# One decoder layer on one core: transposes in PSUM banks of their own, first partial products in scratch tiles, and new list priorities

## The chip, the core and the metric

The kernel runs on one core of a Trainium2 chip. A core has five engines that work side by side, each through its own list of instructions, in order: TensorE (PE in the profile: matrix products and transposes; its weight loads are counted as PEld), VectorE (DVE), ScalarE (ACT), GpSimd (POOL) and SyncE (SP, which here only issues transfers). TensorE writes to PSUM, which has eight banks of 128 x 512 float32; the other engines read it from there. The metric is the device time of one execution in microseconds (us), and the median of three runs is what is compared.

## The reference

The layer takes x (1024 tokens x 1024 channels, float32) and computes

```
h = rms_norm(x) ; z = h @ w_in                  # 2840 columns: q, 6 x (k or v), gates, hc, cg, bg
k_cmp, v_cmp = compress(kc), compress(vc)       # 32-token blocks, stride 16: gelu(blk @ w1 + b1) @ w2 + b2
attn = nsa_attention(q, k_cmp, v_cmp, ks, vs, kw, vw, sigmoid(gates))   # three branches, 8 heads, 2 groups
conv = bg * causal_conv3(cg * hc)               # short gated convolution, 512 channels
x = x + concat(rms_norm(attn), rms_norm(conv)) @ w_o
x = x + square(relu(rms_norm(x) @ w_up)) @ w_down
```

## The kernel before, in words

Every float32 product is three TensorE products of operands split into a high and a low part (`mm3`: high x high, low x high, high x low). So each operand needs an ACT copy (the high part, names in h or `hTh`, `w_hi`, `w1h`, `wcuh`, `MCh`, `KH`) and a DVE subtraction (the low part, `hTl`, `w_lo`, `w1l`, `wcul`, `MCl`, `KL`), and each result in PSUM has to be drained by ACT or DVE before its bank is used again.

The order of the instructions is not that of the code. A planner (`class Plan`) records every operation with what it needs, gives each a modelled cost (`cost`, L288) and a priority (the longest modelled path from it to the end, plus whatever `plan.plus` holds while the operation is written down, L348), and then lists for each engine what is ready first and has the highest priority. For a transfer the model takes its bytes. All instructions are then issued from one line, L268, so the line tells nothing in this profile and the rows are told apart by the names of their tiles: `out<-in`.

PE's stages in this order: norm and transposes of x, and the k/v columns of z (to 77 us); the q columns (`zp`, eight 512-wide PSUM results, each in w_hi/w_lo pieces) mixed with the compression (`compress_steps`: the loads `ch<-kv_d`, the transposes `tp<-ident,ch`, `araw`, `ah`/`al`, and `hp`, the 16 x 3 products with the streamed first weight `w1h`/`w1l`, whose raw tiles `w_raw<-in_w_cmp` have two buffers) to 131 us; a 280-wide rest of z to 156 us; the convolution's channels (`channels`, `u_pair`: a Strassen-like scheme with seven products over the PSUM results `zX`, `zZ`, `zW`, and the weight sums `wcr`, `wcs`) to 277.5 us. There the first products `A11` and `S2` are copied by ACT into the two halves of the tile `u`, and a DVE addition completes them later. Then `wc`, the convolution half of the output projection (`hTh`/`hTl` hold split rows of w_o there, `MCh`/`MCl` the convolution's result): for each of eight blocks of 128 tokens two 512-wide results, each 12 products, drained by DVE with the factor `rconv` (the convolution's norm, from the column sums `s_<-ones,sqs`) onto a tile that x was loaded into: `y` tiles for six blocks, the single buffer `xt` (pool `xq`, bufs=1) for the first two, from where POOL stores them to `x_d` before `xt` is loaded a second time. Mixed with these stand the transposes of the normed keys (`tp<-ident,kn`, split to `KH`/`KL`), those of the queries (`tpq`) and the first scores. From 337 us on: attention, its projection, and the feed-forward part.

PSUM: to the end of the convolution the pool `psB` has five banks under the tag "mm" (z, hp, zX, zZ, zW) and three under "tr" (transposes). Then `psB` is closed, and `psP` (three banks, transposes), `psS` and `psC` (`wc`: tags "ot" x2 and "ms") are opened in its place; a new tile there waits for whatever used the bank last.

Of the kernel before, what the change touches and what calls it, by code (L numbers as in the profile page):

```python
# [9 lines left out]
F32 = mybir.dt.float32  # L10
# [3 lines left out]
ALU = mybir.AluOpType  # L14
# [4 lines left out]
P = 128  # L19
# [131 lines left out]
class Plan:  # L151
# [133 lines left out]
    last_pe = None  # L285
    plus = 0.0
    follow = ()
    LINK = .05  # L288
    GROUP = 1

    def cost(self, name, method, a, kw, views):
        self.port = False
        n = max([v.cols() for _, v in views], default=1)
        psum = any(v.base.pool.psum for k, v in views if k not in ("out", "accum_out"))
        if method == "dma_start":
            nb = 4 * max(int(np.prod(v.shadow.shape)) for _, v in views)
            return (.58 if name == "POOL" else .33), 0.0, nb
        if name == "PE":
            if method == "transpose":
                c = .109  # L300
            else:
                rhs = a[2]
                c = rhs.cols()
                c = max(4 * c / 4560, .218) if rhs.base.args[1] == F32 else max((c if c >= 256 else 4 * c) / 2400 + .014, .109)
            return c, c + .17, 0
        near = not psum
        if name == "ACT":
            c = (.1 if near else .05) + n * .000834
            if any(isinstance(kw.get(k), View) for k in ("scale", "bias")):
                c += .09  # L310
            acc = kw.get("accum_out") is not None
            return max(c, .17) + .093 * acc, max(c, .17) + .11 + .093 * acc, 0
        if name == "DVE":
            if method == "tensor_tensor_reduce":
                return .163 + n * .00104, .26 + n * .00104, 0
            if method == "scalar_tensor_tensor":
                c = .1 + n * .0011 if n >= 200 else .11 + n * .0012
            elif method == "tensor_scalar":
                c = .06 + n * .00059 + (.05 if n < 64 else 0)
            elif method == "memset":  # L320
                c = .08 + n * .0005
            else:
                c = .064 + n * .00104
            self.port = near and n >= 64
            return c, c + .08, 0
        self.port = n >= 64
        if method == "tensor_tensor":
            if kw.get("op") == ALU.pow:
                return .4 + .15 * n, .45 + .15 * n, 0
            c = .15 + n * .00213  # L330
            return c, c + .05, 0
        if method in ("iota", "affine_select"):
            self.port = False
            return .08 + n * .001, .13 + n * .001, 0
        c = .15 + n * .0009 if method == "tensor_copy" else .12 + n * .0008
        return c, c + .05, 0
# [158 lines left out]
def trunk_layer(ctx, tc, x, g_mix_norm, w_in, g_q, g_k, pe_cmp, w_cmp1, b_cmp1, w_cmp2, b_cmp2,  # L495
# [85 lines left out]
    gk_bc = twp.tile([P, 3, HD], F32, name="gk_bc")  # L581
    TD = {n: [htp.tile([P, 4, 512], F32R, name=f"{n}{q}") for q in "hl"] for n in ("t1", "t2")}
    wp = pool(wp_stack, "wp", bufs=4, side="right")
    psB_stack = ExitStack()
    psB = pool(psB_stack, "psB", bufs=5, space=PSUM)

# [25 lines left out]
    with ExitStack() as a:  # L612
# [9 lines left out]
        nc.sync.dma_start(rows[24:36], conv_w.rearrange("j (k p) -> (j k) p", p=P))  # L622
        nc.sync.dma_start(rows[36:68], pe_cmp.rearrange("k (q two) d -> (k q) (two d)", two=2))
        plan.plus = 0.0
        tp = psB.tile([P, 512], F32, name="tp", tag="tr", bufs=3)
        nc.tensor.transpose(tp[:, :68], rows, ident[:68, :68])
        nc.vector.tensor_copy(cols, tp[:, :68])
        def norm_in(tb):
            xt = xts[tb]
            junk = xp.tile([P, D], BF16, name="junk", tag="junk", bufs=1)  # L630
            ss = st.tile([P, 1], F32, name="ss")
            nc.scalar.activation(junk, xt, AF.Square, accum_out=ss)
            ri = st.tile([P, 1], F32, name="ri")
            rsqrt(ri, ss, 1, 1.0 / D)
            nc.vector.tensor_scalar(xt, xt, ri, None, op0=ALU.mult)
            for half in range(2):
                tp = psB.tile([P, 4, P], F32, name="tp", tag="tr", bufs=3)
                for j in range(4):
                    k = half * 4 + j
                    nc.tensor.transpose(tp[:, j], xt[:, k * P:(k + 1) * P], ident)  # L640
                d = (slice(None), slice(half * 4, half * 4 + 4), slice((tb % 4) * P, (tb % 4 + 1) * P))
                split_psum(hTh[tb // 4][d], hTl[tb // 4][d], tp)
# [17 lines left out]
    def z_tokens(pieces, tbs, n, steps=iter(()), per=0):  # L660
        pss = [psB.tile([P, 512], F32, name="zp", tag="mm") for _ in tbs]
        for j, (wh, wl) in enumerate(pieces):
            for ps, tb in zip(pss, tbs):
                t = slice((tb % 4) * P, (tb % 4 + 1) * P)
                for i in range(2):
                    k = 2 * j + i
                    mm3(ps[:, :n], hTh[tb // 4][:, k, t], hTl[tb // 4][:, k, t], wh[:, i], wl[:, i],
                        k == 0, k == KD - 1)
            for _ in range(per):
                plan.plus = 20  # L670
                next(steps, None)
                plan.plus = 0.0
        return list(zip(tbs, pss))
# [44 lines left out]
    with ExitStack() as b1:  # L718
# [40 lines left out]
        def compress_steps():  # L759
            for kv in range(2):  # L760
                yield
                ch = cp.tile([P, 16, HD], F32, name="ch")
                for g in range(G):
                    c0 = kv * G * HD + g * HD
                    nc.sync.dma_start(ch[g * 64:(g + 1) * 64],
                                      kv_d[:, c0:c0 + HD].rearrange("(i p) d -> i p d", p=16))
                A = {}
                for half in range(2):
                    A[half] = (cp.tile([P, 8, P], F32R, name=f"ah{half}"), cp.tile([P, 8, P], F32R, name=f"al{half}"))
                for q4 in range(2):  # L770
                    yield
                    tp = psB.tile([P, 4, P], F32, name="tp", tag="tr", bufs=3)
                    for j in range(4):
                        pp = q4 * 4 + j
                        nc.tensor.transpose(tp[:, j], ch[:, 2 * pp:2 * pp + 2], ident)
# [32 lines left out]
                nc.vector.tensor_scalar(hx, hx, 0.5, None, op0=ALU.mult)  # L808
                nc.vector.scalar_tensor_tensor(hx, th, 1.0, hx, op0=ALU.add, op1=ALU.mult)
                yield  # L810
                tp = psB.tile([P, 4, P], F32, name="tp", tag="tr", bufs=3)
                for j in range(2):
                    nc.tensor.transpose(tp[:, j], hx[:, j * P:(j + 1) * P], ident)
                hT = cp.tile([P, 2, P], F32, name="hT", tag="th")
# [48 lines left out]
                tt(nc.vector, qg[:, :, 1 - g], zg, qg[:, :, g].bitcast(F32), ALU.subtract)  # L863
            nc.sync.dma_start(q_d[tb * P:(tb + 1) * P], qn.rearrange("p h a d -> p (h a d)").bitcast(F32))

        plan.plus = 20
        for _ in steps:
            pass
        plan.plus = 0.0
# [20 lines left out]
    with ExitStack() as b2:  # L890
# [13 lines left out]
        def channels(c0, c1):  # L904
            A = {}
            for j in range(2):
# [7 lines left out]
                for k in range(4):  # L914
                    copy_act(raw[:, k], raw[:, k], scale=cols[:, G_MIX + 4 * j + k:G_MIX + 4 * j + k + 1])
                A[f"A1{j + 1}"], A[f"A2{j + 1}"] = raw[:, :, 0], raw[:, :, 1]
            PART = {"A11": ("b11", "X"), "S1": ("t1", "Z"), "S2": ("t2", "X"), "A12": ("b21", "W"),
                    "S3": ("b12", "X"), "S4": ("b22", "Z"), "A22": ("t4", "X")}
            ps = {}
            for name, (b, chain) in PART.items():  # L920
                hi, lo = [wc.tile([P, 4, P], F32R, name=f"wcu{q}", bufs=3) for q in "hl"]
                copy_act(hi, A[name])
                tt(nc.vector, lo, A[name], hi.bitcast(F32), ALU.subtract)
# [6 lines left out]
                if name == "A12":  # L930
                    tt(nc.vector, A["A12"], A["A12"], A["S2"], ALU.subtract)
                    A["S4"] = A["A12"]
                if chain not in ps:
                    ps[chain] = psB.tile([P, 512], F32, name="z" + chain, tag="mm")
                bh, bl = TD[b]
# [5 lines left out]
        def u_pair(c):  # L941
# [2 lines left out]
            nc.vector.memset(u[:, 0:2], 0.0)  # L944
            for name, ps in channels(C_CONV + c * P, C_CONV + CW + c * P):
                if name == "A11":
                    copy_act(u0, ps)
                elif name == "A12":
                    tt(nc.vector, u0, ps, u0, ALU.add)
                elif name == "S2":  # L950
                    copy_act(u1, ps)
                elif name == "S1":
                    a = half_tile("ca")
                    copy_act(a, ps)
                elif name == "S3":
                    tt(nc.vector, a, ps, a, ALU.add)
                elif name == "S4":
                    tt(nc.vector, u1, ps, u1, ALU.add)
                    tt(nc.vector, u1, u1, a, ALU.mult)
                else:  # L960
                    tt(nc.vector, u0, ps, u0, ALU.mult)
# [59 lines left out]
        for c in range(4):  # L1021
# [4 lines left out]
                copy_act(hi[:, j], r[:, j], scale=g)  # L1026
                nc.vector.scalar_tensor_tensor(lo[:, j], r[:, j], g, hi[:, j].bitcast(F32), op0=ALU.mult, op1=ALU.subtract)
            pieces.append((hi, lo))
        tpk = psB.tile([P, 4, P], F32, name="tpk", tag="tr", bufs=3)
        nc.tensor.transpose(tpk[:, 0], kcn, ident)  # L1030
        wc_stack.close()
        ht_stack.close()
# [39 lines left out]
        def k_transposes(g, br, qd):  # L1072
# [3 lines left out]
            c0 = NCMP + br * T + qd * 512  # L1076
            split_keys(g, c0, 512, tp.rearrange("p a b -> p (a b)"))

        for g in range(G):
            split_keys(g, 0, NCMP, tpk[:, 0, g * 64:(g + 1) * 64])  # L1080
        psB_stack.close()
        cps_stack, psP_stack = ctx.enter_context(ExitStack()), ctx.enter_context(ExitStack())
        psP = pool(psP_stack, "psP", bufs=3, space=PSUM, side="right")
        psC = pool(cps_stack, "psC", space=PSUM, side="right")
        psS_stack = ExitStack()
        psS = pool(psS_stack, "psS", bufs=2, space=PSUM)
# [112 lines left out]
        kts = [(i % 2, i // 2 % 2, i // 4) for i in range(8)]  # L1199
        for i in range(4):  # L1200
            k_transposes(*kts.pop(0))
        for it, tb in [*enumerate(ORDER)][6:] + [*enumerate(ORDER)][:6]:
            xt = xq.tile([P, D], F32, name="xt") if it >= 6 else y_tile([P, D], f"y{tb}")
            nc.sync.dma_start(xt, x2d[tb * P:(tb + 1) * P])
            t = slice(tb * P, (tb + 1) * P)
            for nh in range(2):
                n = slice(nh * 512, (nh + 1) * 512)
                tag, bufs = (("ot", 2), ("ot", 2), ("ms", 1))[(it * 2 + nh) % 3]
                ps = psC.tile([P, 512], F32, name="wc", tag=tag, bufs=bufs)
                for c in range(4):  # L1210
                    wh, wl = pieces[c]
                    mm3(ps, MCh[:, c, t], MCl[:, c, t], wh[:, nh], wl[:, nh], c == 0, c == 3)
# [478 lines left out]
```

## Time and profile before

| | |
|---|---|
| runs | 1247.05, 1249.01, 1251.22 us; median 1249.01 |
| profiled execution | 1247.95 us, of which the span from the first to the last instruction is 1246.2 |
| PE busy | 1210.3 us of the span, 97% |
| DVE, ACT, POOL busy | 927.8, 713.5 and 706.6 us |
| PE waits of over 0.15 us named in the waits view | about 30 us over the whole span |
| mean granted TensorE clock | 0.997 |

The span is about as long as PE's work; a time is read here as PE's busy time and the gaps between its instructions. A gap is put down to the event that came last before the waiting instruction began ("releaser"). [...]

### The profile page before, as it was taken

How to read it: one execution, taken by the hardware profiler on the slowest of the kernel's cores; microseconds unless marked ns; L12 is line 12 of the kernel's file. 1: busy time of each engine (PE TensorE's matmuls, PEld its weight loads, DVE VectorE, ACT ScalarE, POOL GpSimd, SP SyncE). 2: the span in 40 equal slices, each digit the busy share in tenths (PEclk: the TensorE clock that was granted, in tenths of full speed). 3: DMA queues.
4: the chain of work that ended last, by engine and by line, in shares of the span. 5: the costliest groups of instructions: out<-in, count | busy, mean ns of one | idle time of the engine just before them, and what ended most of it. 6: DMA issues, size and time to landing. Idle time of an engine off the chain costs nothing.

```text
span 1246.2 us, 18370 instructions
## 1 busy us (share of the span) xinstructions
PE 1210.3 (97%) x5970; PEld 996.8 (80%) x5970; DVE 927.8 (74%) x1784; ACT 713.5 (57%) x1586; POOL 706.6 (57%) x629
## 2 busy tenths in 40 slices
PE   7989999999989999999999999999999999999998
PEld 6868978777868888888788888888888788888786
DVE  6947766774498789898876665665658999898874
ACT  7557854552388788787956555555344444444440
POOL 2435410011235554333768777877889999888860
PEclk9999999999999999999999999999999999999999
DMA  6265622138121100001225534445349545554413
GB/s 242 64 152 176 179 59 68 42 93 257 58 93 43 38 31 35 27 18 37 100 93 177 178 121 166 135 145 178 136 146 402 184 163 170 168 169 120 134 43 135
DMA packets 105175, 155.01 MB, mean 124 GB/s; under 512 B 20404, under 2 KB 59400, under 8 KB 105080
## 3 DMA queue, kind: packets, MB, share of 16 engines
q1 hardware_dynamic: 102008, 146.05, 36.2%
q10 hardware_dynamic: 2304, 5.24, 1.1%
q0 software_dynamic: 768, 2.56, 0.7%
q8 instruction: 47, 0.77, 0.3%
q14 instruction: 48, 0.39, 0.1%
HBM read 106.63 MB, written 47.19 MB: 123 GB/s over the span
## 4 chain that ended last, share of the span: by engine, by line
PE 75%; DVE 6%; DMA 5%; ACT 5%; issue 3%; POOL 2%; SPq 0%; ACTq 0%; DVEq 0%; POOLq 0%
PE X L268 24%; PE Z L268 15%; PE tp L268 5%; PE ot L268 4%; PE zX L268 4%; PE wa L268 4%; PE wc L268 3%; PE W L268 3%; PE zp L268 2%; PE zZ L268 2%; DMA wu<-in_w_up_dram 2%; PE zW L268 1%; DVE y L268 1%; PE hp L268 1%; POOL d L268 1%
## 5 line engine op out<-in xcount | busy, mean ns | idle before, releaser
L268 PE MATMUL X<-we,uu 128*128 128x512 f32 x720 | 179.5, 390 | 2.0 <-DVE y L268 2.0
L268 PEld LDWEIGHTS X<-we,uu 128*128 128x128 f32 x720 | 134.5, 188 | 32.2 <-ACT uu L268 3.0
L268 PE MATMUL Z<-we,uu 128*128 128x512 f32 x576 | 146.4, 390 | 0.0
L268 ACT ACTIVATE uu<-ur 128x512 fp32r<-128x512 f32 x108 | 66.7, 630 | 121.2 <-PE X L268 58.3
L268 PEld LDWEIGHTS Z<-we,uu 128*128 128x128 f32 x576 | 107.5, 188 | 24.2 <-issue 1.1
L268 ACT ACTIVATE pt<-pt,nm 128x640 f32<-128x640 f32 (+7 forms) x128 | 93.8, 736 | 27.6 <-DVE nm L268 27.1
L268 PE MATMUL tp<-ident,pt 128*128 128x128 f32 x528 | 103.4, 273 | 1.4 <-DVE pl L268 1.1
L268 POOL TENSOR_TENSOR d<-d 128x512 f32<-128x512 f32 x64 | 98.2, 1555 | 10.1 <-DVE d L268 8.1
L268 ACT ACTIVATE ph<-tp 128x512 fp32r<-128x512 f32 (+1 forms) x148 | 82.1, 575 | 31.4 <-PE tp L268 29.0
L268 DVE TENSOR_TENSOR pl<-tp,ph 128x512 fp32r<-128x512 f32 (+1 forms) x148 | 94.7, 654 | 7.2 <-ACT ph L268 6.7
L268 DVE TENSOR_TENSOR y<-X,y 128x512 f32<-128x512 f32 x128 | 79.6, 680 | 13.6 <-PE X L268 13.5
L268 POOL TENSOR_TENSOR uu<-ur,uu 128x512 fp32r<-128x512 f32 x54 | 77.6, 1442 | 12.4 <-DVE y L268 8.7
L268 DVE TENSOR_TENSOR uu<-ur,uu 128x512 fp32r<-128x512 f32 x54 | 72.1, 1349 | 13.1 <-ACT uu L268 12.5
L268 DVE TENSOR_TENSOR we<-s,we 128x512 fp32r<-128x512 f32 x42 | 38.5, 916 | 57.5 <-PE Z L268 25.0
L268 PEld LDWEIGHTS tp<-ident,pt 128*128 128x128 f32 x528 | 68.6, 140 | 13.7 <-POOL pt L268 1.4
L268 DVE TENSOR_TENSOR y<-Z,y 128x512 f32<-128x512 f32 x96 | 61.3, 682 | 19.7 <-PE Z L268 19.6
L268 ACT ACTIVATE wu<-wu,cols 128x256 f32<-128x256 f32 x128 | 55.7, 502 | 24.0 <-DMA wu<-in_w_up_dram 23.5
L268 ACT ACTIVATE we<-wu 128x512 fp32r<-128x512 f32 x57 | 35.9, 631 | 57.5 <-PE X L268 43.9
L268 DVE SCALAR_TENSOR_TENSOR d<-d 128x512 f32<-128x512 f32 x48 | 65.2, 1359 | 0.8
L268 POOL IOTA d_sw<- 128x640 f32 (+1 forms) x2 | 1.2, 609 | 113.3 <-PE zZ L268 113.3
L268 PE MATMUL zp<-w_lo,hTh 128*128 128x512 f32 (+1 forms) x192 | 62.0, 368 | 0.3 <-DVE w_lo L268 0.3
L268 POOL TENSOR_TENSOR pt<-pt,rr 128x640 f32<-128x640 f32 (+4 forms) x64 | 62.3, 1004 | 0.0
(1333 smaller groups left out, 3689.7 us busy)
## 6 DMA issues: line engine op xcount, KB each, us to landing
u_d<-d SPq DMA_DIRECT2D x112, 256.0 KB, 3.2
ur<-u_d SPq DMA_DIRECT2D x108, 256.0 KB, 2.9
wu<-in_w_up_dram SPq DMA_DIRECT2D x16, 1024.0 KB, 6.1
wd<-in_w_down_dram SPq DMA_DIRECT2D x16, 1024.0 KB, 6.3
xt<-in_x_dram SPq DMA_DIRECT2D x10, 512.0 KB, 4.9
w_raw<-in_w_in_dram SPq DMA_DIRECT2D x8, 512.0 KB, 5.9
w_raw<-in_w_cmp_dram SPq DMA_DIRECT2D x16, 256.0 KB, 3.0
q_d<-qn SPq DMA_DIRECT2D x8, 512.0 KB, 3.1
```

Source lines behind the costliest of these rows:

```text
L268: node.do.append(lambda: getattr(engine, method)(*[real(x) for x in a], **{k: real(x) for k, x in kw.items()}))
```

## The change

Six edits, none of which adds or removes an instruction. (1) While the two `ch` loads of each compression are recorded, the planner takes their bytes 2.4 times (`drag`). (2) The pool `psP` with three banks is opened at the start and all transposes take their bank from it until the end of the attention; `psB` is left with five. (3) The compression steps that are written between the q pieces have `plan.plus` 6 in place of 20, and so has what is left of them at the end. (4) The weight loads, sums and splits in `channels` have `plan.plus` 6 in place of 0. (5) `A11` and `S2` go to scratch tiles `ta` and `tb`, one buffer each, and the completing additions read these. (6) The first split of compressed keys has `plan.plus` 20, and the first two `wc` results (the two halves of one token block) take banks of `psP`.

```diff
@@ cost
-            return (.58 if name == "POOL" else .33), 0.0, nb
+            return (.58 if name == "POOL" else .33), 0.0, int(nb * self.drag)
@@
+    psP_stack = ctx.enter_context(ExitStack())
+    psP = pool(psP_stack, "psP", bufs=3, space=PSUM, side="right")
     psB_stack = ExitStack()
     psB = pool(psB_stack, "psB", bufs=5, space=PSUM)
@@ the transposes of rows, x, ch, hx and kcn alike
-                tp = psB.tile([P, 4, P], F32, name="tp", tag="tr", bufs=3)
+                tp = psP.tile([P, 4, P], F32, name="tp", tag="pt")
@@ z_tokens, and again where the rest of the steps is written
-                plan.plus = 20
+                plan.plus = 6
                 next(steps, None)
@@ compress_steps
+                    plan.drag = 2.4
                     nc.sync.dma_start(ch[g * 64:(g + 1) * 64],
                                       kv_d[:, c0:c0 + HD].rearrange("(i p) d -> i p d", p=16))
+                    plan.drag = 1.0
@@ channels
+            plan.plus = float(6)
             PART = {"A11": ("b11", "X"), "S1": ("t1", "Z"), "S2": ("t2", "X"), "A12": ("b21", "W"),
...
             for name, (b, chain) in PART.items():
+                plan.plus = float(6)
...
+                plan.plus = 0.0
                 if chain not in ps:
@@ u_pair
                 if name == "A11":
-                    copy_act(u0, ps)
+                    t0 = wc.tile([P, 512], F32, name="ta", bufs=1)
+                    copy_act(t0, ps)
                 elif name == "A12":
-                    tt(nc.vector, u0, ps, u0, ALU.add)
+                    tt(nc.vector, u0, ps, t0, ALU.add)
                 elif name == "S2":
-                    copy_act(u1, ps)
+                    t1 = wc.tile([P, 512], F32, name="tb", bufs=1)
+                    copy_act(t1, ps)
...
-                    tt(nc.vector, u1, ps, u1, ALU.add)
+                    tt(nc.vector, u1, ps, t1, ALU.add)
@@ after the convolution
+        plan.plus = 20.0
         for g in range(G):
             split_keys(g, 0, NCMP, tpk[:, 0, g * 64:(g + 1) * 64])
+        plan.plus = 0.0
         psB_stack.close()
-        cps_stack, psP_stack = ctx.enter_context(ExitStack()), ctx.enter_context(ExitStack())
-        psP = pool(psP_stack, "psP", bufs=3, space=PSUM, side="right")
@@ the wc loop
-                ps = psC.tile([P, 512], F32, name="wc", tag=tag, bufs=bufs)
+                if wc_done < 2:
+                    ps = psP.tile([P, 512], F32, name="wc", tag="pt")
+                else:
+                    ps = psC.tile([P, 512], F32, name="wc", tag=tag, bufs=bufs)
+                wc_done += 1
```

Each engine has as many instructions as before. PE's order is the same up to the last pieces of q before the first `ch` transposes (77 us in the trace of before), and again the same from 332 us to the end; the other engines' orders part and join at about the same places.

Place one, PE, where the compression's first transposes stand among the q products. Before:

```order
L268 MATMUL zp<-w_lo,hTh_124 128x512 x2
L268 MATMUL zp<-w_hi,hTl_123 128x512 x2
L268 MATMUL zp<-w_hi,hTh_124 128x512 x2
L268 MATMUL tp<-ident,ch 128x128 x8
L268 MATMUL zp<-w_lo,hTh_124 128x512 x2
```

With the change:

```order
L268 MATMUL zp<-w_hi,hTh_124 128x512 x2
L268 MATMUL zp<-w_lo,hTh_124 128x512 x2
L268 MATMUL zp<-w_hi,hTl_123 128x512 x2
L268 MATMUL zp<-w_hi,hTh_124 128x512 x2
L268 MATMUL zp<-w_lo,hTh_124 128x512 x2
L268 MATMUL zp<-w_hi,hTl_123 128x512
L268 MATMUL tp<-ident,ch 128x128 x8
L268 MATMUL zp<-w_hi,hTh_124 128x512
```

Counted from the row of two `w_hi,hTh` that ended the q products before, nine more of them (2 + 2 + 2 + 2 + 1) now stand ahead of the eight transposes.

Place two, PE, from the last product of the convolution to the first output products and key transposes (`hTh_169` of before is `hTh_172` with the change, `kn_2986` and `kn_2988` are `kn_2990` and `kn_2992`). Before:

```order
L268 MATMUL zX<-t4h,wcul 128x512
L268 MATMUL wc<-hTh_169,MCh 128x512 x2
L268 MATMUL wc<-hTl_168,MCh 128x512 x2
L268 MATMUL wc<-hTh_169,MCl 128x512 x2
...
L268 MATMUL s__3037<-ones,sqs_2124 128x1 x4
L268 MATMUL s__3037<-ones,sqs_2123 128x1 x3
...
L268 MATMUL tp<-ident,kn_2986 128x128 x3
L268 MATMUL tp<-ident,kn_2988 128x128
```

With the change:

```order
L268 MATMUL zX<-t4h,wcul 128x512
L268 MATMUL wc<-hTh_172,MCh 128x512 x2
L268 MATMUL wc<-hTl_171,MCh 128x512
L268 MATMUL tp<-ident,kn_2990 128x128 x2
L268 MATMUL wc<-hTl_171,MCh 128x512
L268 MATMUL wc<-hTh_172,MCl 128x512
L268 MATMUL tp<-ident,kn_2990 128x128 x2
...
L268 MATMUL wc<-hTh_172,MCh 128x512 x3
...
L268 MATMUL s__3045<-ones,sqs_2143 128x1 x4
L268 MATMUL s__3045<-ones,sqs_2142 128x1 x4
```

The first key transposes have moved from behind the column sums to among the first output products. From the last `zX` to the sums there were 24 products of `wc`; there are now 44 of `wc` and 12 transposes.

Place three, SP, the loads around the first x tile of the output projection. Before:

```order
L268 DMA y_2991<-in_x_dram 128x1024
L268 DMA xt<-in_x_dram 128x1024
L268 DMA kn_2989<-k_d_189 128x2x64 x8
L268 DMA y_3162<-in_x_dram 128x1024
L268 DMA qx<-q_d 128x512
L268 DMA vs<-v_ds 128x8x256
L268 DMA y_3176<-in_x_dram 128x1024
L268 DMA vw<-v_dw 128x8x256
```

With the change:

```order
L268 DMA y_2995<-in_x_dram 128x1024
L268 DMA kn_2993<-k_d_192 128x2x64 x8
L268 DMA y_3106<-in_x_dram 128x1024
L268 DMA qx<-q_d 128x512
L268 DMA vs<-v_ds 128x8x256
L268 DMA vw<-v_dw 128x8x256
L268 DMA xt<-in_x_dram 128x1024
L268 DMA y_3211<-in_x_dram 128x1024
```

The first `xt` load now stands behind the last eight key loads, one `y` load, the queries and both value loads.

## Rows read from the trace of the kernel before

**Rows 1.** Page, busy time, share of the span and instructions by engine.

```profile
PE 1210.3 (97%) x5970; PEld 996.8 (80%) x5970; DVE 927.8 (74%) x1784; ACT 713.5 (57%) x1586; POOL 706.6 (57%) x629
```

**Rows 2.** Waits, PE, whole span: us in total, times, longest us.

```profile
PE tp L268 <- DMA ch<-kv_d: 3.3, 1, 3.3
PE wc L268 <- DVE cv L268: 2.2, 1, 2.2
...
PE zX L268 <- ACT u L268: 1.6, 2, 1.1
PE hp L268 <- ACT ah L268: 1.5, 1, 1.5
PE tp L268 <- DVE KL L268: 1.2, 2, 1.1
...
PE zZ L268 <- ACT wcuh L268: 1.2, 1, 1.2
...
PE hp L268 <- DVE w1l L268: 0.7, 1, 0.7
...
PE wc L268 <- DVE y L268: 0.6, 2, 0.3
...
PE wc L268 <- DVE xt L268: 0.4, 1, 0.4
```

**Rows 3.** Windows: busy time by engine (x instructions), then PEclk, DMA share, GB/s.

```profile
78.40:81.80 3.40, 3.40 (x10) 2.73 (x9) 0.77 (x2) 2.69 (x14) 1.80 (x2) 0.50 0.75 133
...
279.80:283.20 3.40, 3.40 (x8) 2.72 (x9) 3.37 (x7) 2.05 (x5) 1.73 (x3) 0.50 0.43 96
291.50:296.20 4.70, 3.38 (x26) 2.57 (x24) 2.85 (x5) 2.21 (x5) 0.00 (x0) 1.00 0.62 154
359.70:363.10 3.40, 1.39 (x11) 0.94 (x9) 3.33 (x7) 0.69 (x2) 3.40 (x3) 1.00 0.00 0
```

**Rows 4.** Timeline of PE: start, us, operation and count, idle before.

```profile
77.02 1.06 PE L268 MATMUL tp<-ident,ch 128*128 128x128 f32 x8 [3.30 <-DMA ch<-kv_d]
...
99.64 0.40 PE L268 MATMUL zp<-w_hi,hTl 128*128 128x512 f32 x1
99.87 0.40 PE L268 MATMUL zp<-w_lo,hTh 128*128 128x512 f32 x1
...
277.16 0.39 PE L268 MATMUL zX<-t4h,wcul 128*128 128x512 f32 x1
...
291.48 1.47 PE L268 MATMUL tp<-ident,kn 128*128 128x128 f32 x12
```

**Rows 5.** The tile w_raw, 60 to 131 us: loads of the compression's weight.

```profile
L268 SPq DMA_DIRECT2D w_raw<-in_w_cmp_dram x16: 367/368/858, 68.1 to 120.4; - x16
```

**Rows 6.** Timeline of DVE around the end of the convolution.

```profile
279.06 0.68 DVE L268 TENSOR_TENSOR cv<-zX,cv 128x512 f32<-128x512 f32 x1
279.66 0.68 DVE L268 TENSOR_TENSOR MCl<-cv,MCh 128x512 fp32r<-128x512 f32 x1
...
282.00 0.45 DVE L268 TENSOR_TENSOR KL<-tpk,KH 64x64 fp32r<-64x64 f32 x2
...
283.13 2.49 DVE L268 TENSOR_TENSOR sqs<-sqs,cv 128x512 f32<-128x512 f32 x4
...
293.29 2.12 DVE L268 TENSOR_TENSOR KL<-tp,KH 64x512 fp32r<-64x512 f32 x3 [4.09 <-ACT KH L268]
295.34 1.39 DVE L268 SCALAR_TENSOR_TENSOR xt<-wc,rconv,xt 128x512 f32<-128x512 f32 x2
```

**Rows 7.** Landing, us min/median/max: stores of x_d, y loads, vw load.

```profile
DMA to landing us min/median/max: 2.9/5.7/8.5
...
DMA to landing us min/median/max: 3.9/7.9/14.4
...
DMA to landing us min/median/max: 13.6/13.6/13.6
```

**Rows 8.** Page, DMA issues: times issued, KB each, median us to landing.

```profile
xt<-in_x_dram SPq DMA_DIRECT2D x10, 512.0 KB, 4.9
```

More of the change, by code (lines that the diff above doesn't have):

```diff
@@ L287 @@
     follow = ()
+    drag = 1.0
     LINK = .05
@@ L624, in trunk_layer @@
         plan.plus = 0.0
-        tp = psB.tile([P, 512], F32, name="tp", tag="tr", bufs=3)
+        tp = psP.tile([P, 512], F32, name="tp", tag="pt")
         nc.tensor.transpose(tp[:, :68], rows, ident[:68, :68])
@@ L771, in compress_steps @@
                     yield
-                    tp = psB.tile([P, 4, P], F32, name="tp", tag="tr", bufs=3)
+                    tp = psP.tile([P, 4, P], F32, name="tp", tag="pt")
                     for j in range(4):
@@ L810, in compress_steps @@
                 yield
-                tp = psB.tile([P, 4, P], F32, name="tp", tag="tr", bufs=3)
+                tp = psP.tile([P, 4, P], F32, name="tp", tag="pt")
                 for j in range(2):
@@ L864, in trunk_layer @@
             nc.sync.dma_start(q_d[tb * P:(tb + 1) * P], qn.rearrange("p h a d -> p (h a d)").bitcast(F32))
-        plan.plus = 20
+        plan.plus = 6
         for _ in steps:
@@ L1028, in trunk_layer @@
             pieces.append((hi, lo))
-        tpk = psB.tile([P, 4, P], F32, name="tpk", tag="tr", bufs=3)
+        tpk = psP.tile([P, 4, P], F32, name="tpk", tag="pt")
         nc.tensor.transpose(tpk[:, 0], kcn, ident)
@@ L1077, in k_transposes @@
             split_keys(g, c0, 512, tp.rearrange("p a b -> p (a b)"))
+        plan.plus = 20.0
         for g in range(G):
             split_keys(g, 0, NCMP, tpk[:, 0, g * 64:(g + 1) * 64])
+        plan.plus = 0.0
         psB_stack.close()
-        cps_stack, psP_stack = ctx.enter_context(ExitStack()), ctx.enter_context(ExitStack())
-        psP = pool(psP_stack, "psP", bufs=3, space=PSUM, side="right")
+        cps_stack = ctx.enter_context(ExitStack())
         psC = pool(cps_stack, "psC", space=PSUM, side="right")
@@ L1201, in trunk_layer @@
             k_transposes(*kts.pop(0))
+        wc_done = 0
         for it, tb in [*enumerate(ORDER)][6:] + [*enumerate(ORDER)][:6]:
```

## The prediction

> **What bounds the kernel now.** I read the busy line first: PE works 1210.3 us of a span of 1246.2 [rows 1], so 36 us of PE gaps are all that a new order can touch, and since the change moves work only between 77 and 332 us, only the gaps there count. I read next the waits of PE [rows 2]. In that stretch stand `ch` 3.3, `ah` 1.5 and `w1l` 0.7 (compression); `u` 1.6 and `wcuh` 1.2 (convolution); `cv` 2.2, the first output product; and behind it `KL` 1.2, `y` 0.6 and `xt` 0.4. Together 12.7 us. [...]
>
> **Part one, the compression (77 to 131 us).** Nine q products now stand ahead of the first `ch` transposes. Two of them start 0.23 us apart (99.64 and 99.87, [rows 4]), so they cover 9 x 0.23 = 2.1 of the 3.3 us, and 1.2 remain. The loads are issued at about the same time, since SP's order is the same up to there. With a gap of 1.2 us I take the clock drop that followed (1.7) to go too: the stretch from 291.5 to 296.2, where PE did nearly only transposes and stood still for 1.3 us, was at 1.00 [rows 3]. Further on, the `hp` products are spread out between more q products, so the waits for `ah` and `w1l` (2.2 together) lose their sharpness; I leave 1.0 for one that stays or comes new. Before 3.3 + 1.5 + 0.7 + 1.7 = 7.2; after 1.2 + 1.0 = 2.2; gain 5.0. Bounds: nothing, if the waits only change places, and 7.2.
>
> **Part two, the convolution (131 to 277 us).** `A11` and `S2` were held up because the tile `u` has an earlier user; the three waits for `u` and `wcuh` are 2.8 us [rows 2]. A scratch tile of one buffer is free as soon as the addition of the pair before has read it, which is a whole pair (some 30 us) earlier. The copies themselves, their engine and their length don't change, so there is no new work. I leave 0.8 for an ACT queue that is still late once: gain 2.0, bounds 0 and 2.8. The priority of 6 for the weight sums moves DVE and ACT instructions earlier, in stretches where DVE's cover is PE's own work. If that pushes a drain back by one 512-wide operation, it costs 0.6 (279.06 to 279.66, [rows 6]); that is inside the 0.8.
>
> **Part three, the junction (277 to 287 us).** The first `wc` result waited 2.2 us until DVE had added the last `zX` (at 279.06, though its last product began at 277.16 [rows 4, 6]), since it was to have that bank. In `psP` it has no such wait. What is late next is DVE's queue behind that point: the addition and two `MCl` (0.6 each), two `hTl` (0.7 each, as the two operations of this kind at 295.34), three `sqs` (2.49 / 4 = 0.62 each) and two `KL` (2.12 / 3 = 0.7 each): 1.8 + 1.4 + 1.9 + 1.4 = 6.5 us, from rows 6, which starts late by 1.5 (277.55 to 279.06) and now has the two small `KL<-tpk` (0.45) ahead of it: 8.5 us. The third and fourth `wc` results need the banks that those last two `KL` read. Ahead of them on PE stand 20 `wc` and 12 transposes: 20 x 0.23 + 12 x 0.12 (1.47 us for 12, [rows 4]) = 6.0. So PE stands 2.5 us there, in pieces between products, and not in one piece: I take the clock to stay. Before 2.2 + 1.7 = 3.9, after 2.5: gain 1.4; bounds -0.7 (clock falls all the same, and 0.4 more of DVE) and 3.9 (DVE not late).
>
> **Part four, the rest of the output projection (287 to 332 us).** This is where the change takes. The eight column sums stand behind 44 `wc` products where they stood behind 24. The load of the first `xt` may begin only after them (it lies where the sums' inputs lay), and SP now issues it behind eight key loads, `y`, `qx`, `vs` and `vw`. From the sums to the transpose that needs the bank of its drained result PE has 38 `wc` and 12 transposes, 38 x 0.23 + 12 x 0.12 = 10.1 us. An `xt` load takes 4.9 in the median [rows 8]; but `vw`, which is now just ahead of it, took 13.6 from issue to landing [rows 7]. From 4.9 no wait comes; from 13.6, with 0.3 for SP and 0.74 for the drain (1.39 for two, [rows 6]), 4.6. I take 1.0, nearer to the median because the load is one of ten of that kind. Then the chain of the single buffer: the second drain 0.7, POOL's store (0.6 to issue, 2.9 to 8.5 to land [rows 7]), SP 0.3, the second `xt` load (4.9 [rows 8] to 7.9, the middle of the `y` loads [rows 7]), its drain 0.7: 10.1 to 18.7 us. PE has 20 `wc`, 16 transposes and 4 scores to do until it needs that drain, 20 x 0.23 + 16 x 0.12 + 4 x 0.2 = 7.3, and about 0.8 of small waits: 8.1. So a wait of 2.0 to 10.6; I take 2.0, since the store of before whose landing took 2.9 is the one that had no value load ahead of it. The small waits for `KL` and `y` (1.8 before) I leave as they are: 1.8 + 1.0 + 2.0 = 4.8 after, 2.2 before; loss 2.6. Bounds: nothing, and 1.8 + 4.6 + 10.6 - 2.2 = 14.8.
>
> **The sum.** 5.0 + 2.0 + 1.4 - 2.6 = 5.8 us. From 332 us on the order is the same on every engine and PE is what bounds, so the lead carries to the end. The profiled execution took 1247.95 (1.75 around its span) and the median of the runs is 1249.01, 1.06 above. 1247.95 - 5.8 = 1242.15 for that execution, 1243.2 for a median.
>
> **Rivals.** *The clock falls in both places all the same* (two times 1.7, so 1246.6). For it: both drops of before came right behind a gap; the gap before `ch` is still 1.2 with eight transposes behind it. Against it: 291.5 to 296.2, and the 2.0 us gap at 359.7 to 363.1 (PE busy 1.39 of 3.40), both at 1.00 [rows 3]. [...]
>
> *The compression is paced by its weight loads.* Sixteen `w_raw` loads are issued from 68.1 to 120.4 us, one in 3.3 [rows 5], into two buffers that ACT and DVE must have read. Then what PE saves at `ch` it gives back at the `hp` products, and the change doesn't do in this stretch what it says: part one falls to 0, and 1243.2 + 5.0 = 1248.2. Against it: if the loads set the pace, PE would wait for many of the sixteen pieces; it waits once for `w1l`, 0.7 us [rows 2], so 3.3 us is PE's own pace.
>
> *Slower: the single `xt` buffer decides.* Load 1 lands like `vw` (13.6), the store like the slower one (8.5), load 2 like a `y` (7.9): 17.0 us of waits in part four, and with PE quiet for ten of them one drop of the clock, 1.7. 17.0 + 1.7 - 2.2 = 16.5 lost against 8.4 gained ahead of it: 8.1 slower, 1257.1. It decides from the point where part four's waits pass 8.4 + 2.2 = 10.6 us. For it: the load is issued behind `vs` and `vw`, where it stood ahead of them. Against: the transfers are moved as a group, with PE ahead of them by the lead, and the second store of before landed in 2.9 [rows 7]. [...]
>
> **How the numbers follow.** The forecast 0.58; the clock 0.11; the weight loads 0.14; the single buffer 0.14, of which some ends between 1247 and 1253; something else 0.03. The likeliest case's own range goes from 1239 (parts one and three at their better ends, part four at 2 lost) to 1247 (part one at 2, the rest as forecast, and 0.8 more). The range for 8 in 10 takes in the clock and the weight loads and the smaller half of the last: 1238 to 1251. What a measurement can tell from no change is 0.3%, 3.7 us, so faster is below 1245.3 and slower above 1252.8. Of the forecast's 0.58 about 0.50 lies below 1245.3, and 0.05 comes from the clock falling once only and from the rest: 0.55. The same holds the weight loads, the rest of the clock and of the forecast and a third of the single buffer: 0.31. Slower: 0.14.
>
> **What would show it.** In the profile after: the wait for `ch` at about 1.2, and the window behind it at clock 1.00; no waits for `u` above 0.5; the first `wc` right behind the last `zX`, and some 2 to 3 us of waits for `hTl` and `KL` behind it, at clock 1.00; then a wait for `xt` twice, 1 and 2 us; and PE's start into attention about 6 us earlier. It is wrong if an `xt` wait passes 5 us, if the clock falls at either place, if the `hp` products wait 3 us or more for `w1l` or `ah`, or if after 332 us PE gives the lead back.

## The result, and the profile after

The changed kernel took 1239.06 us (median of 6 runs, 1236.59 to 1242.5) against 1249.26 (6 runs, 1246.83 to 1251.22): a ratio of 0.9919, 95% interval 0.9898 to 0.9941. Measured again later on one chip with other variants it took 1240.46 against 1248.17, a ratio of 0.9939 (0.9924 to 0.9954). So it is faster by 7.7 to 10.2 us in the medians, where 5.8 were forecast. (A ratio given here isn't formed from the two medians, so what it makes in us can differ from the medians' difference by 1 or 2 us.) One of the six executions of experiment 4's kernel took 2009.38 us at a mean granted clock of 0.557; it is left out of the figures. The changed kernel's profiled execution took 1240.24 (before: 1247.95), 7.7 less.

The busy times on the page, after, answer to [rows 1]:

```profile
PE 1206.8 (97%) x5970; PEld 994.6 (80%) x5970; DVE 931.5 (75%) x1784; ACT 714.4 (58%) x1586; POOL 701.5 (57%) x629
```

PE's waits from 71 us to the start of the attention, after, answer to [rows 2], with the same columns:

```profile
PE tp L268 <- DVE xt L268: 2.3, 1, 2.3
PE tp L268 <- DMA ch<-kv_d: 1.4, 1, 1.4
PE zp L268 <- ACT w_hi L268: 1.0, 1, 1.0
PE wc L268 <- DVE KL L268: 1.0, 1, 1.0
PE wc L268 <- DVE xt L268: 0.6, 1, 0.6
PE tp L268 <- DVE KL L268: 0.5, 1, 0.5
PE wc L268 <- DVE hTl L268: 0.5, 1, 0.5
PE wc L268 <- DVE y L268: 0.4, 1, 0.4
```

The waits for `u`, `wcuh`, `ah`, `w1l` and `cv` are gone; `ch` is down from 3.3 to 1.4; a wait for `xt` of 2.3 has come. The clock, as a share of full speed, in windows of the same kernel (behind `ch`, at the first `wc`, behind the wait for `xt`), answers to [rows 3]:

```profile
76.90:80.30 3.40, 3.39 (x20) 2.99 (x21) 0.97 (x3) 1.26 (x2) 1.88 (x2) 1.00 0.53 158
267.00:271.20 4.20, 4.20 (x25) 3.31 (x24) 4.10 (x8) 3.27 (x7) 3.11 (x7) 1.00 0.45 100
297.30:301.70 4.40, 4.40 (x18) 3.85 (x19) 2.73 (x4) 1.20 (x2) 1.21 (x2) 0.61 0.49 180
```

It stays at 1.00 in the two places where it fell before, and falls in a third, to 0.61 in the mean of 4.4 us: 4.4 x 0.39 = 1.7 us are lost there, an estimate from the granted clock. The chain behind that, in the timelines of SP, DVE and PE:

```profile
284.38 0.58 SPq L268 DMA_DIRECT2D vw<-v_dw  x1
285.08 3.24 SPq L268 DMA_DIRECT2D xt<-in_x_dram  x1
...
296.50 1.41 DVE L268 SCALAR_TENSOR_TENSOR xt<-wc,rconv,xt 128x512 f32<-128x512 f32 x2 [4.15 <-DMA xt<-in_x_dram]
...
297.30 0.33 PE L268 MATMUL tp<-ident,kn 128*128 128x128 f32 x1 [2.34 <-DVE xt L268]
```

The load issued behind `vw` at 285.08 lands 11.3 us later, when DVE starts, and a key transpose waits for the bank that DVE drains. The issue alone held SP for 3.24 us; that of the second `xt` load, at 301.31, took 0.33.

To compare kernels I use the stretch in which the orders differ, from PE's last common q products to the first product of the attention (`ot`). Before, and after:

```profile
71.50:343.80 272.30, 259.01 (x1284) 212.45 (x1283) 176.54 (x369) 144.23 (x428) 58.81 (x63) 0.99 0.40 118
```

```profile
71.20:334.80 263.60, 255.72 (x1285) 211.33 (x1283) 178.57 (x371) 145.55 (x428) 53.73 (x63) 0.99 0.41 122
```

It takes 8.7 us less: PE's idle time falls from 13.3 to 7.9 (5.4), the low clock from 3.4 us lost to 1.7 (1.7), and the rest, 1.6, is PE's busy time at the full clock. Behind the stretch the profiled execution of after took 1.3 us longer than that of before, 1.0 of it a new wait of the queries' transposes (`tpq`) for a `qx` load. So the lead isn't carried to the end whole.

### The profile page after: what moved, and what is told of

Same layout as the page of the kernel before. It is cut to its first block, busy times and chain, and to the rows that moved or that the text cites. A ratio compares the mean times of both kernels' runs of the same rounds, so it can differ in the third digit from the quotient of the medians.

```text
span 1238.5 us, 18368 instructions
## 1 busy us (share of the span) xinstructions
PE 1206.8 (97%) x5970; PEld 994.6 (80%) x5970; DVE 931.5 (75%) x1784; ACT 714.4 (58%) x1586; POOL 701.5 (57%) x629
## 4 chain that ended last, share of the span: by engine, by line
PE 82%; DVE 5%; DMA 5%; ACT 2%; issue 1%; POOL 1%; DVEq 0%; ACTq 0%; SPq 0%; POOLq 0%
PE X L268 26%; PE Z L268 16%; PE zX L268 5%; PE tp L268 5%; PE zp L268 5%; PE ot L268 4%; PE wa L268 4%; PE W L268 4%; PE zZ L268 3%; PE wc L268 2%; DMA wu<-in_w_up_dram 2%; PE zW L268 1%; DMA xt<-in_x_dram 1%; PE hp L268 1%; DVE y L268 1%
## 5 line engine op out<-in xcount | busy, mean ns | idle before, releaser
L268 PE MATMUL zp<-w_hi,hTh 128*128 128x512 f32 (+1 forms) x192 | 61.0, 367 | 1.2 <-ACT w_hi L268 1.2
```

Source lines behind the costliest of these rows:

```text
L268: node.do.append(lambda: getattr(engine, method)(*[real(x) for x in a], **{k: real(x) for k, x in kw.items()}))
```

## The experiments

Each kernel was run in five rounds beside the kernel before: experiments 1 to 4 on one chip, 5 to 8 on a second, 9 to 12 on a third, so kernels from different groups are compared by their ratios. The stretch of the profiled execution is given too, because the rest of the execution, where the orders are much the same, varies by up to 5.8 us between the profiles.

**1. The compression's edits alone.**

```diff
+                    plan.drag = 2.4      # the ch loads
...
-                plan.plus = 20
+                plan.plus = 6            # z_tokens, and the rest of the steps
```

> The kernel before with the compression's two edits alone (ch loads dragged 2.4 times in the model, step priority 6 in place of 20). Theory (the gain is a sum of separate places): the wait for ch falls from 3.3 to about 1.4 us, those for ah and w1l (2.2) go, one of about 1 comes, and the clock stays at 1.00 behind ch (1.7): 4.8 us in the named waits, so about 1244 us; the waits for u, wcuh and cv stay as they were. Rival (the lead only moves the waits on): the same wait for ch, but the lead of some 5 us at the end of the compression is smaller by 3 or more at the first wc product, and the time is above 1247.

1241.98 against 1247.48, ratio 0.9947 (0.9928 to 0.9967): 5.5 us in the medians, 6.6 by the ratio. The stretch takes 264.9. `ch` 1.7, no wait for `ah` or `w1l`, `w_hi` 1.0 new; `u` 1.0, `wcuh` 1.2 and `cv` 1.3 are left of 1.6, 1.2 and 2.2. The clock behind `ch`:

```profile
79.20:83.20 4.00, 3.94 (x22) 3.42 (x23) 1.51 (x3) 1.26 (x2) 2.42 (x2) 1.00 0.62 161
```

The theory of separate places holds, with more than its 4.8; the lead isn't given back. At the junction the clock still falls, as before (0.50 from 282.9 to 286.2).

**2. The bank edits alone.**

```diff
+    psP = pool(psP_stack, "psP", bufs=3, space=PSUM, side="right")   # all transposes
...
+        plan.plus = 20.0                                             # first key split
...
+                if wc_done < 2:
+                    ps = psP.tile([P, 512], F32, name="wc", tag="pt")
```

> The kernel before with the bank edits alone (psP open from the start for all transposes, the first two wc results in it, the first key split at priority 20). Theory of separate places: ch waits 3.3 us and u and wcuh 2.8 as before; the 2.2 us wait of the first wc goes, the clock stays at 1.00 there (1.7), and 1 to 1.5 us of waits for hTl and KL come. As the first xt load stands ahead of the value loads in this kernel, there is no xt wait of over 0.5: 2.5 us faster than before, 1246.7. Rival: the three banks that transposes have to themselves shorten the compression too; then the waits for ah and w1l change and the time is 1245 or less.

1249.57 against 1247.48, ratio 1.0012 (0.9996 to 1.0028): no gain. Both expectations fell. The first `wc` no longer waits for `cv`, but `hTl` holds PE for 1.8 us, and the clock is low for far longer than before, at `ch` and at the junction:

```profile
79.00:84.60 5.60, 5.57 (x18) 4.84 (x19) 1.46 (x3) 3.56 (x17) 2.13 (x2) 0.50 0.67 155
285.80:296.80 11.00, 10.55 (x38) 8.93 (x39) 4.64 (x9) 1.68 (x3) 1.64 (x1) 0.53 0.54 165
```

By the granted clock these windows lose 2.8 and 5.2 us, against 1.7 in each of the two places before (3.4 us at 0.50). It is so in the other executions too: the twelve have a mean granted clock of 0.9942 (0.992 to 0.996), the 23 of the kernel before beside them 0.9971 (0.995 to 1.000), and 0.0029 of 1246 us is 3.6 us, an estimate that takes PE as busy meanwhile, as it is in these windows. So the wait went as the theory said, and the low clock took back more than that was worth. Why it lasts longer in this kernel isn't shown.

**3. The scratch tiles alone.**

```diff
-                    copy_act(u0, ps)
+                    t0 = wc.tile([P, 512], F32, name="ta", bufs=1)
+                    copy_act(t0, ps)          # and so for u1, with tb
```

> The kernel before with the scratch tiles ta and tb alone. Theory: the two waits for u (1.6 us) go, that for wcuh (1.2) may stay, since its priority is as before; nothing else changes: 1 to 3 us faster, about 1247.2. Rival: the copies were not held by the tile u but by ACT's own queue; then waits of 1.6 us stay under another name and the time is as before, 1249.

1244.33 against 1247.48, ratio 0.997 (0.9956 to 0.9984): 3.2 us in the medians, 3.7 by the ratio, above what was expected. There is no wait for `u`, and none for `wcuh` either, which had its priority of before: it stood behind the copies. ACT where PE waited for `wcuh`, before and then with the scratch tiles:

```profile
219.51 0.60 ACT L268 ACTIVATE u<-zX 128x512 f32<-128x512 f32 x1
220.02 0.63 ACT L268 ACTIVATE wcuh<-wcr 128x512 fp32r<-128x512 f32 x1
```

```profile
218.20 0.62 ACT L268 ACTIVATE wcuh<-wcr 128x512 fp32r<-128x512 f32 x1
...
220.33 0.58 ACT L268 ACTIVATE ta<-zX 128x512 f32<-128x512 f32 x1
```

The largest waits of this kernel in the stretch are `ch` 3.0 (with 6.8 us of low clock behind it), then:

```profile
PE wc L268 <- DVE hTl L268: 2.3, 1, 2.3
PE tp L268 <- DVE KL L268: 1.2, 2, 1.1
```

**4. The value loads behind the first xt load** (in the changed kernel).

```diff
-        for br in "sw":
-            nc.sync.dma_start(V[br]..., v_d[br]...)
...
+            if it == 6:
+                plan.follow = (ld,)       # ld: the first xt load
+                for br in "sw":
+                    nc.sync.dma_start(V[br]..., v_d[br]...)
```

> The changed kernel with the two value loads written behind the first xt load, so that SP issues them after it; all else as in the changed kernel. Theory (the first xt load is late because it stands behind vs and vw in SP's queue): it lands in 4 to 6 us in place of 11.3, the 2.3 us wait of a key transpose for the drain of xt goes, and with it the half clock behind it (1.7 us), the second xt wait (0.6) at most stays: 4 us faster than the changed kernel, about 1235. Rival (the load is slow because all the key, y and query loads share the engines): it still lands in 9 us or more, and the time is within 1 us of the changed kernel's 1239. Second rival (the store and reload of the single buffer decide): the first wait goes, the second grows to 2 us, 1237.5.

1239.84 against 1247.48, ratio 0.9924 (0.9905 to 0.9944), not to be told from the changed kernel. SP and DVE:

```profile
283.68 0.36 SPq L268 DMA_DIRECT2D xt<-in_x_dram  x1
...
289.10 1.41 DVE L268 SCALAR_TENSOR_TENSOR xt<-wc,rconv,xt 128x512 f32<-128x512 f32 x2 [5.26 <-DMA xt<-in_x_dram]
```

The load lands in 5.4 us in place of 11.3, as the theory says, yet PE waits 2.0 us, and the clock falls behind it (0.56 in the window below): the planner also listed the transposes that need the bank earlier. From the column sums to the waiting transpose PE has 16 products and 4 transposes here, and 38 and 12 in the changed kernel.

```profile
289.90:293.60 3.70, 3.69 (x15) 3.22 (x16) 3.58 (x6) 1.79 (x3) 0.61 (x1) 0.56 1.00 312
```

**5. The change without the drag.**

```diff
-                    plan.drag = 2.4
+                    plan.drag = 1.0
```

> The changed kernel with the drag of the ch loads taken back to 1.0; step priority 6 and all other edits stay. Theory (the nine q products that the drag puts ahead of the transposes carry most of part one): the wait for ch is 3.0 to 3.3 us again and the clock falls behind it, so 1.9 + 1.7 = 3.6 us of the changed kernel's gain go, or more if the low clock lasts longer; ratio to before about 0.995. Rival (priority 6 carries it, by spreading the hp products): ratio 0.992 as with the change.

1244.72 against 1248.41, ratio 0.9974 (0.9956 to 0.9992). `ch` 3.0 and the low clock behind it (3.4 us) are back, as expected. So is a wait for `cv` of 2.6, at the second product of `wc`, with a second low clock behind it (3.4 us, from 276): the order behind shifted, though the bank edits are in this kernel, and why it waits there isn't shown. The stretch takes 267.4, 3.8 more than with the change, so not all of the loss is the drag's own place.

**6. A drag of 4.0.**

```diff
-                    plan.drag = 2.4
+                    plan.drag = 4.0
```

> The changed kernel with a drag of 4.0 in place of 2.4: some nine more q products stand ahead of the first ch transposes. Theory: they cover the 1.4 us wait that is left, nothing waits for ch, 1.4 us faster than the changed kernel, ratio to before about 0.991. Rival (the compression's tail is late for what stands behind it): the ch wait goes, but hp, cps or the 280-wide piece wait 1.4 us or more later, ratio 0.992 or higher.

1243.29 against 1248.41, ratio 0.9962 (0.995 to 0.9974). Ten more q products than with 2.4 stand ahead of the transposes and nothing waits for `ch`, but the kernel is no faster and by its ratio slower: `w_hi` holds the 280-wide rest of z for 1.3 us with the clock low behind it (0.51 in the window below), and the second `xt` costs 1.3. The rival is right; the interval touches that of the changed kernel's second measurement.

```profile
124.00:127.30 3.30, 3.18 (x12) 2.83 (x13) 2.54 (x7) 3.11 (x16) 0.14 (x1) 0.51 0.18 34
```

**7. The change without the bank edits** (experiment 2's lines taken back).

> The changed kernel without the bank edits (transposes in psB's three banks as before, the first wc results in psC, the first key split at its own priority); drag, step priority, channel priority and scratch tiles stay. Theory (parts one and two carry the gain; the bank edits only trade one wait for others): the first wc waits about 2 us with a drop of the clock, no xt wait of over 0.5 us; ratio to before 0.991 to 0.993, as with the change. Rival (the bank edits pay once the rest is out of the way, by 1.4 us or more): ratio 0.9935 or higher.

1240.25 against 1248.41, ratio 0.9937 (0.9926 to 0.9949). The changed kernel has 0.9919 and 0.9939 in its two measurements, so in it the bank edits are worth nothing that shows. By the ratio alone the rival's bound of 0.9935 is passed; the interval holds both. `cv` 2.3 with a low clock behind it (3.4 us), `xt` 0.9 in two; stretch 261.9. Experiments 1 and 3 gave 5.5 and 3.2 us in the medians, 8.7 together; this kernel has both and the priority of 6 in `channels`, and gives 8.2. So those two places add up, and nothing is left that this priority would have to explain; no run has it alone.

**8. Two xt buffers** (in the changed kernel).

```diff
-        xq = pool(b2, "xq", bufs=1, side="right")
+        xq = pool(b2, "xq", bufs=2, side="right")
```

> The changed kernel with two buffers for the xt tiles in place of one, so the second load needs no store to land; both loads then stand ahead of the value loads in SP's list. Theory (the two xt waits and the clock behind the first cost 2.3 + 0.6 + 1.7 us): the second wait is gone, the first load lands in 4 to 6 us; as PE's list asks for its drain earlier too, a wait of 1 to 2 us may stay: 2 to 4 us faster than the changed kernel, ratio 0.989 to 0.990. Rival (the wait only moves, as it did with the value loads behind the first xt load): ratio 0.992.

1238.07 against 1248.41, ratio 0.9923 (0.9911 to 0.9934). The second wait is gone. The first load lands in 5.6 us, but the first wait is 2.2 us, again with a low clock behind it (3.4 us), and `hTl` costs 1.6: the wait moved, as in experiment 4. Only 27 products and 6 transposes stand between the column sums and the product that waits.

**9. The changed kernel again.**

> The changed kernel itself, unedited, beside the next three on the same chip. Theory: from 71 us to the first product of the attention it takes 263.6 us as before, of which 2.3 and 0.6 are waits for xt and 1.7 the low clock behind the first; ratio to before 0.992. Rival (the low clock behind the xt wait is chance, and was in the one profiled execution): no low clock there and 262 us.

1240.46 against 1248.17, ratio 0.9939 (0.9924 to 0.9954). The time in the stretch is the rival's, but not for its reason alone: in this execution the first load lands in 9.6 us in place of 11.3, so the wait itself is smaller. PE's two waits for `xt`:

```profile
PE wc L268 <- DVE xt L268: 1.2, 1, 1.2
...
PE tp L268 <- DVE xt L268: 0.5, 1, 0.5
```

The clock stays up there; but it falls behind the 2.0 us wait for `nm` early in the attention, where it hadn't before [rows 3]:

```profile
295.90:300.30 4.40, 4.10 (x22) 3.30 (x23) 2.71 (x5) 1.08 (x2) 1.21 (x2) 1.00 0.62 198
353.00:357.90 4.90, 4.90 (x22) 3.88 (x20) 4.39 (x14) 4.46 (x10) 1.44 (x3) 0.65 0.27 104
```

The stretch takes 261.9, 1.7 less than in the first profile.

**10. The xt loads dragged by 3** (in the changed kernel).

```diff
+            plan.drag = 3.0 if it >= 6 else 1.0
             nc.sync.dma_start(xt, x2d[tb * P:(tb + 1) * P])
+            plan.drag = 1.0
```

> The changed kernel with the planner taking the two xt loads' bytes three times, so that it lists their drains, and what needs the banks of these, later; nothing else. Theory (the xt waits and the low clock behind them are what part four costs): both waits under 0.5, clock at 1.00 there: 3 to 4.5 us less from 71 us to the first product of the attention, 259 to 260.5, ratio to before about 0.989. Rival (what is listed in their place waits instead, for y, KL or the reload): the stretch takes 262 us or more, ratio 0.992.

1238.37 against 1248.17, ratio 0.992 (0.9905 to 0.9934). One `xt` wait of 0.4 is left and the clock stays up in the stretch, which takes 260.3: 1.6 to 3.3 less than the changed kernel's two profiles. The waits go as the theory says (40 products and 16 transposes now stand ahead of the one that waits). Of the size about half shows, since the changed kernel doesn't lose the clock each time; the medians differ by 2.1 us (1240.46 - 1238.37) and the intervals overlap, so the gain in time is likely and not shown.

**11. Two xt buffers and the drag of 3.**

> The changed kernel with two xt buffers and the planner taking their loads' bytes three times. Theory: no reload chain and no early need: no xt wait of over 0.3, clock at 1.00, what is left are ch (1.1), w_hi (1.0) and hTl and KL (1.6): 256.5 to 258 us in the stretch, ratio to before about 0.987. Rival (the waits move on, as with two buffers alone): 260 us, ratio 0.991.

1235.28 against 1248.17, ratio 0.9898 (0.9883 to 0.9913): faster than the changed kernel beside it (1240.46) by 5.2 us, and the fastest here. The whole stretch and the window at the junction, then its waits of PE:

```profile
72.40:329.20 256.80, 252.59 (x1284) 209.79 (x1283) 178.31 (x369) 145.58 (x428) 53.63 (x63) 1.00 0.43 125
...
273.50:277.50 4.00, 3.84 (x23) 2.94 (x23) 3.97 (x8) 1.21 (x3) 0.00 (x0) 1.00 0.44 99
```

```profile
PE tp L268 <- DMA ch<-kv_d: 1.6, 1, 1.6
PE zp L268 <- ACT w_hi L268: 1.6, 2, 1.0
PE wc L268 <- DVE hTl L268: 1.5, 1, 1.5
```

No wait for `xt`, `KL` or `y`, no low clock in the stretch, and 256.8 as the theory had it.

**12. The same without the bank edits.**

> As the kernel before this one, but without the bank edits (transposes in psB, first wc results in psC). Theory (the bank edits trade the first wc's wait and its low clock, 2.3 + 1.7, for waits behind hTl and KL of 1.6): slower than with them by 2 us, 259 to 260 us in the stretch. Rival (the bank edits are worth nothing or less): 257.5 us or less.

1239.94 against 1248.17, ratio 0.9932 (0.9917 to 0.9947); stretch 262.8. The theory's direction is right and its size too small: without their banks, `cv` 2.3, `KL` 2.1 and `hTl` 0.5 are waited for. The low clock that the theory counted behind `cv` (1.7) didn't come in the profile:

```profile
PE wc L268 <- DVE cv L268: 2.3, 1, 2.3
PE tp L268 <- DVE KL L268: 2.1, 3, 1.1
```

```profile
271.80:275.20 3.40, 2.81 (x11) 2.02 (x12) 3.35 (x6) 1.63 (x4) 0.72 (x2) 1.00 0.43 99
```

So the bank edits are worth 4.7 us in the medians (1239.94 - 1235.28) once `xt` isn't in the way, nothing that shows in the changed kernel, and nothing alone, where the low clock takes it. Whether one of the two `xt` edits would do to bring them out wasn't tried.

## Why the prediction was right, and where its sizes were off

**Direction and places.** The mechanism was right: most of the gain comes out of PE's gaps and the low clock in the stretch, and 1239.06 and 1240.46 are inside the range, below the point by 4.1 and 2.7. By their named waits, parts two and three gained more than forecast, part one about as much, and part four lost a little more.

**Part one, the compression.** 2.2 us of waits were left in the sum; 1.4 and 1.0 are measured, and the clock stayed up. Alone it gave 5.5 to 6.6 us where 5.0 stood. That the clock stays up behind so short a wait came true in all nine profiles with a `ch` wait of 0.8 to 1.8 us, but it isn't safe: it fell behind the 1.3 us wait of experiment 6. The drag carries over half of what the whole change gains: without it the ratio is 0.9974.

**Part two, the convolution.** 0.8 of 2.8 us was left for "an ACT queue that is still late once"; nothing is left in the profile after. The scratch tiles alone gave 3.2 to 3.7 us where 2.0 stood, and took the `wcuh` wait along with the ones for `u` (experiment 3), since that operation only stood behind the held copies.

**Part three, the junction.** DVE's queue was what was late next, as the sum had it, but 1.5 us of waits came (`hTl` 0.5, `KL` 1.0) in place of 2.5, so this gain is the one mis-sized most by proportion, 2.4 for 1.4. The last `zX` ended at 267.25 and the next `wc` result could start at 275.27, when the first of three `KL` (from 274.54) was done: 8.0 us of DVE where 8.5 stood, with two `KL` in the sum. PE's 20 products and 12 transposes took the other 6.6 us, where 6.0 stood. The clock held, with the waits in pieces as the sum had it; in experiments 8 and 11, with one piece of 1.6 and 1.5, it held too, and in experiment 2, with one of 1.8, it fell.

**Part four, the rest.** The named chain is there: the `xt` load behind `vw` took 11.3 us, between the 4.9 and the 13.6 of the bounds. 4.8 us of waits were forecast, 3.9 came (`xt` 2.3 and 0.6, `KL` 0.5, `y` 0.4). What the sum had not is the low clock behind the first `xt` wait, 1.7 us in the first profile and none in the second. The second profile had 0.5 and 1.2 for `xt`. The reload after the store cost 0.6 and 1.2 in place of 2.0: the store landed in 3.0 us in the first profile. Two sums there are off by rounding and nothing hangs on them: 38 x 0.23 + 12 x 0.12 is 10.2, and the wait from 13.6 is 4.5.

**The sum.** By these terms, with what was measured in them, the profiled executions differ by 7.2 - 2.4 = 4.8 in part one, 2.8 in part two, 3.9 - 1.5 = 2.4 in part three and 2.2 - 3.9 - 1.7 = -3.4 in part four: 6.6 us, and 7.1 by the stretch's idle time and low clock, which count every small gap. The stretch gained 8.7. The 1.6 us of busy time at full clock stay unexplained: by the same working (busy time less what the low clock took) the other profiles give 252.6 to 255.4 us and before 255.6, so it may be that one execution. The first comparison's 10.2 in the medians against 7.7 in the profiles may be such variation too: measured again the medians differ by 7.7. The 1.7 that parts one and three count for each drop of the clock is half of a 3.4 us window at 0.50 [rows 3]; in the first of these products of 512 columns start 0.43 us apart (two take the 0.85 us from 78.39 to 79.24) and 0.23 apart at 1.00 [rows 4], by which the window costs 1.6 us, an estimate. The clock's own share was counted too high: the sum has it back whole, 3.4 us, while over the executions of the third group the mean granted clock is 0.9985 with the change and 0.9969 before, which is 2.0 us.

**The rivals.** In the two profiles of the changed kernel the clock fell in neither of its two places; the window from 76.9 in the first shows eight transposes behind a 1.4 us wait at 1.00. It fell in a third place in one profile and in a fourth in the other. The weight loads did not pace the compression: no `w1l` or `ah` wait is left. The single buffer didn't decide, though its load was late for the reason given: behind `vs` and `vw` it landed in 11.3 and 9.6 us, ahead of them in 5.4 (experiment 4). But the buffer, with the list that trusts it, hides what the bank edits are worth (experiments 7, 11 and 12).

## What to carry to other kernels

An edit that removes a wait and shows no gain may be covered by the next wait, or by a lower clock: look at both, and measure it again with the next wait taken away, as the bank edits here went from nothing to 4.7 us. Where a planner sets the order, a transfer that lands late is better told to the planner than only issued earlier, for the planner uses the earlier time at once (experiments 4 and 8 against 10 and 11). A larger drag isn't better: 2.4 left 1.4 us of the wait, and 4.0 removed it without a gain. And with a planner each edit lists anew what stands behind it (experiment 5), so that a difference of 1 or 2 us belongs to the list that came out and not surely to the edit.

## What the runs showed of the hardware that was not expected

The low clock doesn't come in one size or each time. Behind a wait for `ch` of 3.0 to 3.3 us it came in all four profiles that have one, for 3.4 us in two (before [rows 3] and experiment 5) and for 6.8 us in two (experiments 2 and 3); behind the junction it lasted 10.2 us in experiment 2. Behind the same 2.0 us wait for `nm` it fell, for 3.4 us each time, in eight of the thirteen profiles other than experiment 1's and stayed up in five, and the changed kernel has one of each. Behind the nine waits of 0.8 to 1.8 us for `ch` in the other profiles it never fell, but it did behind 1.3 us for `w_hi` (experiment 6). In experiments 1 and 3 it fell right behind the column sums (0.50 from 282.9 to 286.2 and 0.54 from 286.2 to 289.6), some 1.7 us of products of one column each (in the changed kernel the sixteen of 281.12 to 282.82), with no wait of over 0.6 us just before them. So one profile's count of low stretches, 1.7 us or more apiece, is worth less than the waits beside it; the mean granted clock of all executions says which kernels lose more by it (0.994 in experiment 2, 0.9985 with the change).
